# Low parts on another engine, and a shorter chain of sums and stores, in a one-core encoder layer

## The chip, the cores and the metric

The kernel runs on one core of a Trainium2 chip. A core has TensorE (matrix products, into the accumulator memory PSUM), VectorE, ScalarE and GpSimd (written POOL) for elementwise work, and SyncE (SP), which here only issues transfers. Each engine works through its own list of instructions in order, and semaphores tie the lists together. Transfers run on 16 DMA engines, which the lists of SP, ScalarE or POOL feed. The metric is the device time of one execution in microseconds (us).

## The reference: what is computed

One encoder layer for 512 positions of width 1024, all in float32 (shortened):

```python
x = x + 0.5 * swiglu(rms_norm(x, ffn1_norm), ffn1_w_gate, ffn1_w_up, ffn1_w_down)
h = rms_norm(x, mix_norm)
u = h @ w_in
f_out = fourier_mixer(u[..., :o0], fnet_w, fnet_b)
a_out = gqa_attention(u[..., o0:o1], u[..., o1:o2], u[..., o2:], q_norm, k_norm)
x = x + jnp.concatenate([f_out, a_out], axis=-1) @ w_out
x = x + 0.5 * swiglu(rms_norm(x, ffn2_norm), ffn2_w_gate, ffn2_w_up, ffn2_w_down)
return rms_norm(x, final_norm)
```

`swiglu(h, g, u, d)` is `(silu(h @ g) * (h @ u)) @ d`, with a hidden width of 2752. `rms_norm` divides each position by the root of the mean of its squares over the 1024 channels and multiplies by a gain per channel. The change touches the first FFN and the end of the second one with the final norm.

## The kernel before, in words

**Layout.** The activations lie with channels on the 128 partitions: `x[k]` is chunk k of the channels (8 chunks), 128 x 512. A norm's sum over the channels is therefore a product with a vector of ones.

**Exact products.** A float32 operand is split into a high part, rounded to the form that TensorE multiplies in one pass, and a low part, the rest. A product takes three passes (lines 108 to 110, or line 330): high by high, high by low, low by high. The high part is a cast, mostly on ScalarE. The low part is made in one of two ways. `lows` (line 71) is one VectorE subtraction. `rest_by_dma` (lines 89 to 92) has ScalarE write the negated high part into the low part's place, and then POOL issue a transfer that adds the source onto it:

```python
nc.scalar.activation(lo, asf(hi), AF.Copy, scale=-1.0)
nc.gpsimd.dma_start(out=lo, in_=src, accum_op=ALU.add)
```

**The first FFN's opening.** The hidden chunks come in groups (`GROUPS`). Most gate and up products go by a scheme with seven products of half size for eight (`seven`). It needs h in blocks and seven combinations of them, made by `operands` (lines 242 to 263) in four pairs i = 0 to 3: VectorE writes the scaled blocks of h into a tile b (line 248, two instructions a pair), and differences into a tile t (line 255); ScalarE casts b and t to high parts in `rt` (line 258); then come the low parts. For b in the first FFN that is `rest_by_dma`, for t and for the second FFN `lows`. The tile b has two buffers, so pair 2 takes the buffer of pair 0 when all that read it are done, a transfer included. Meanwhile TensorE runs the first gate and up blocks as plain products (`gate`), each weight block with a high and a low part in two slots of a ring; from the fourth block on these low parts come by `rest_by_dma` too (lines 100, 91, 92), straight from the weights in HBM. So POOL's queue holds transfers for weight blocks and for b in turn. `evacuate` (lines 489 to 510) takes the blocks' results out of PSUM. After the last plain block come the down products of the first group, then the seven products of the next.

**The end.** The last three output chunks of the second FFN (d = 5, 6, 7) are made in two halves of positions by `closing`: first positions 0 to 255 for all three, then positions 256 to 511. After each, `residual` (line 416, VectorE) adds the product to x and `square` (line 134, ScalarE) squares it. The sums of squares of the earlier chunks lie in `n3.acc`. For the first half, the tile acc and two tiles of squares are summed with `ones` (line 157): two columns of 128 positions, three tiles, two passes each. A float32 product without the split takes two passes. This and the mean (line 164, VectorE), the power -1/2 (line 171, POOL), and the copy to a wide tile (line 176) are `column`, which stands between the products of the second half, after their third step of 18. Each step has three passes. `finish` stands after the eighth step: transposes (line 184), a copy to `rb` (line 186, ScalarE), six multiplies by VectorE (line 965) and two by POOL for chunks 2 and 3 (line 963), and four stores of two chunks each in the order 0, 2, 4, 6, all issued by SP (line 968). For the second half, acc and the square of d = 6 are summed ahead of the last square, then the last square; each of the two columns has a PSUM bank and a mean of its own; then come the power, `rows` (products with the identity, lines 196 and 197), and again the multiplies and four stores.

**What sets the order.** Inside the two FFNs the orders of TensorE and SP are as written in the program (`in_order`). The orders of VectorE, ScalarE and POOL are set by a planner that fills each engine by a model of the times and the order of the program; it may place any instruction of these engines anew when any part of the program changes.

Of the kernel before, what the change touches and what calls it, by code (L numbers as in the profile page):

```python
# [8 lines left out]
BF16 = mybir.dt.bfloat16  # L9
# [4 lines left out]
P = 128  # L14
S = 512
D = 1024
KD = D // P
# [25 lines left out]
def encoder(ctx, tc, A, out):  # L43
    nc = tc.nc
# [7 lines left out]
    def bank(name):  # L52
        return pp.tile([P, S], F32, tag="bank", name=name)
# [3 lines left out]
    xt = cp.tile([P, KD, S], F32, name="xt")  # L57
# [12 lines left out]
    def lows(lo, src, hi):  # L70
        nc.vector.tensor_tensor(out=lo, in0=src, in1=asf(hi), op=ALU.subtract)  # L71
# [17 lines left out]
    def rest_by_dma(lo, hi, src):  # L89

        nc.scalar.activation(lo, asf(hi), AF.Copy, scale=-1.0)
        nc.gpsimd.dma_start(out=lo, in_=src, accum_op=ALU.add)
# [19 lines left out]
    class Norm:  # L112
# [39 lines left out]
            self.power(c0, c1)  # L152
            self.spread(c0, c1)

        def sum(self, ps, c, parts, first=True, last=True):
            for i, p in enumerate(parts):
                nc.tensor.matmul(
                    ps[:, 2 * c : 2 * c + 2], p[:, c * P : (c + 1) * P], ones,
                    start=first and i == 0, stop=last and i == len(parts) - 1,
                )  # L160

        def mean(self, ps, c0, c1):
# [17 lines left out]
        def row(self, c0=0, c1=4):  # L180

            ps = bank(f"rp{self.n}_{c0}")
            for c in range(c0, c1):
                nc.tensor.transpose(ps[:, c * P : (c + 1) * P], self.wide[:, c, :], ident)
            t = slice(c0 * P, c1 * P)
            nc.scalar.copy(self.rb[:, t], ps[:, t])
            return ps

        def rows(self, c0, c1):
# [8 lines left out]
            return pss[0]  # L198

    def ffn(norm, after, wgu, wd, wdt, opening, closing):  # L200

        n_ = norm.n
        n_plain = len(GROUPS[0])
        with tc.tile_pool(name=f"act{n_}", bufs=1) as ap, tc.tile_pool(name=f"sums{n_}", bufs=2) as sp:
# [36 lines left out]
            def operands(rp, i0, i1):  # L244
                for i in range(i0, i1):
                    b = sp.tile([P, 4, HALF], F32, tag="raw_g", name=f"b{n_}_{i}")
                    for o, k in ((0, i), (2, i + KH)):
                        nc.vector.scalar_tensor_tensor(
                            out=b[:, o : o + 2].rearrange("p a b -> p (a b)"), in0=x[k],
                            scalar=gains[:, norm.n, k : k + 1], in1=rp, op0=ALU.mult, op1=ALU.mult,  # L250
                        )
                    b12, b11, b22, b21 = (b[:, o] for o in range(4))
                    t = sp.tile([P, 4, HALF], F32, tag=("s12", "s34")[i % 2], bufs=1, name=f"t{n_}_{i}")
                    for o, (p, q) in enumerate(((b12, b11), (b22, t[:, 0]), (b22, b12), (b21, t[:, 1]))):
                        nc.vector.tensor_tensor(out=t[:, o], in0=p, in1=q, op=ALU.subtract)
                    for src, c in ((b[:, 1:], slice(0, 3)), (t, slice(3, 7))):
                        h, l = rt[:, c, 0, i], rt[:, c, 1, i]
                        nc.scalar.copy(h, src)
                        if src is t or n_:
                            lows(l, src, h)  # L260
                        else:
                            rest_by_dma(l, h, src)
# [158 lines left out]
            for gi, group in enumerate(GROUPS):  # L421
                last = gi == len(GROUPS) - 1
# [3 lines left out]
                else:  # L426
# [3 lines left out]
                    pss = dict(enumerate(opening(gate, lambda: norm.column([norm.acc]), lambda: row.append(norm.row()))))  # L430
                    back(lent[:2])
                    due, parts, left = [*pss, "t"], list(range(KH)), range(2 * len(pss), 2 * n_plain)
# [25 lines left out]
                for d in range(KD):  # L458
                    if last and closing and d == KD - 3:
                        closing([(e, down(e, group, gi)) for e in range(d, KD)], residual)  # L460
                        break
                    if last and d == KD - 2:
                        back(lent)
                    ps = bank(f"dn{n_}_{d}_{gi}")
                    steps = down(d, group, gi)(ps, every)
                    for _ in range(len(group) - (last and d < 2)):
                        next(steps)
                    waiting.append((d, ps, steps))
                    if d == 1 and not last:
                        ready = prepare(GROUPS[gi + 1][0] + 1)  # L470
                        ahead.extend(ready[1])
                    if d == 0:
                        rest()
                        if last:

                            lent = slots[KD - 2 : KD]
                            plain[2:2] = lent
                            continue
                    for d_, ps, steps in waiting:
                        for _ in steps:  # L480
                            pass
                        added(d_, ps)
                    waiting = []
# [49 lines left out]
    ident = cp.tile([P, P], F32, name="ident")  # L533
# [39 lines left out]
    with tc.tile_pool(name="mix", bufs=1) as mp, tc.tile_pool(name="mixt", bufs=1) as mt:  # L573

        more = mp.tile([P, 2, KD * P], F32R, name="more")
        more = [more[:, i, :] for i in range(2)]
# [26 lines left out]
        banks, rots, sqs = {}, {}, {}  # L603
# [191 lines left out]
        prob, parts, outs, pair, zs = {}, {}, {}, {}, {}  # L795
# [123 lines left out]
        def attend(n):  # L919
# [7 lines left out]
            if n >= 6:  # L927
                values(*at(n - 6))

        whole = sum(c for c, _, _ in fill)  # L930
        done = 0.0
        for n in range(38):
# [7 lines left out]
        for d in range(KD):  # L940
            whi, wlo = weights(A["wo"][d], f"o{d}")
            ps = bank(f"out{d}")
# [8 lines left out]
    n3 = Norm(3)  # L951

    ready = (2, 3)

    def finish(c0, c1, row=n3.row):

        t = slice(c0 * P, c1 * P)
        pr = row(c0, c1)
        for k0 in range(0, KD, 2):
            for k in (k0, k0 + 1):  # L960
                y = x[k][:, t]
                if k in ready:
                    nc.gpsimd.tensor_tensor(out=y, in0=y, in1=n3.rb[:, t], op=ALU.mult)
                else:
                    nc.vector.scalar_tensor_tensor(
                        out=y, in0=y, scalar=gains[:, 3, k : k + 1], in1=pr[:, t], op0=ALU.mult, op1=ALU.mult
                    )
            nc.sync.dma_start(out=out[:, k0 : k0 + 2, t], in_=xt[:, k0 : k0 + 2, t])

    def closing(downs, residual):  # L970

        for k in ready:
            nc.scalar.activation(x[k], x[k], AF.Copy, scale=gains[:, 3, k : k + 1])
        t0, t1 = slice(0, S // 2), slice(S // 2, S)
        sqs = []

        def more(sq, t):
            nc.vector.tensor_tensor(out=n3.acc[:, t], in0=n3.acc[:, t], in1=sq[:, t], op=ALU.add)

        for d, steps in downs:  # L980
            ps = bank(f"last{d}0")
            for _ in steps(ps, t0):
                pass
            residual(d, ps, t0)
            sq = n3.square(d, t0)
            if d == downs[0][0]:
                more(sq, t0)
            else:
                sqs.append(sq)
        i = 0  # L990
        for d, steps in downs:
            ps = bank(f"last{d}1")
            for _ in steps(ps, t1):
                i += 1
                if i == 3:
                    n3.column([n3.acc, *sqs], 0, 2)
                if i == 8:
                    finish(0, 2)
            if d < KD - 1:
                residual(d, ps, t1)  # L1000
                sq = n3.square(d, t1)
                if d == downs[0][0]:
                    more(sq, t1)
        pss = [bank(f"ss3_{c}") for c in (2, 3)]
        for c, pc in zip((2, 3), pss):
            n3.sum(pc, c, [n3.acc, sq], last=False)
        residual(KD - 1, ps, t1)
        sq = n3.square(KD - 1, t1)
        for c, pc in zip((2, 3), pss):
            n3.sum(pc, c, [sq], first=False)  # L1010
        for c, pc in zip((2, 3), pss):
            n3.mean(pc, c, c + 1)
        n3.power(2, 4)
        finish(2, 4, n3.rows)

    with in_order():
        ffn(n2, n3, A["wgu2"], A["wd2"], A["wdt2"], lambda gate, column, row: [[gate(0, {KD - 1: column}), gate(1, {3: row})]], closing)
# [104 lines left out]
```

## Time and profile before

| what | value |
|---|---|
| three runs | 880.9, 881.03, 880.14 us; median 880.9 us |
| the profiled execution | 880.02 us, of which the span from the first to the last instruction is 878.0 us |
| granted TensorE clock | 0.996 of full speed over the span |
| busy share | PE 98%, DVE 73%, ACT 52%, POOL 4% |
| transfers through POOL's queue | 2560 packets, 4.99 MB |
| bytes moved | 89.25 MB, 102 GB/s on average |

The profile is of one execution. PE is TensorE and PEld its weight loads, DVE is VectorE, ACT is ScalarE; SPq and POOLq are the parts of these engines that issue transfers and wait on semaphores. A line of the order of time has the start and the length in us, the engine, the line of the kernel, the operation, the tiles written and read, the shapes and the count; in brackets follows how long the engine stood idle just before, and what ended that. A line of the waits has who waited for whom, the total in us, the times and the longest. A line of the page's groups has the busy time in us and the mean of one in ns, and behind the second bar the idle time before them and what ended it. Ends of TensorE's passes are modelled.

### The profile page before, as it was taken

Reading aid. Unit: us, or ns where it says so; the run is one execution under the profiler, and the core shown is the slowest. Engines: PE = TensorE matmul, PEld = TensorE weight load, DVE = VectorE, ACT = ScalarE, POOL = GpSimd, SP = SyncE. Lnnn points to the kernel's source line nnn. Section 1 sums busy time; section 2 is a strip of 40 time slices with the busy share of each in tenths; the row PEclk is TensorE's granted clock in tenths of the full one; section 3 lists DMA queues with packets and bytes.
Section 4 is the critical chain, followed back from the end, with each engine's and each line's share of the span. In section 5 each row is a group of like instructions: output and inputs, shape, how many; then the busy total and the mean of one; then the engine's idle time right before and its main releaser. Section 6 shows DMA issues by size and latency. Waiting matters only on the chain.

```text
span 878.0 us, 13599 instructions
## 1 busy us (share of the span) xinstructions
PE 862.1 (98%) x5394; PEld 768.8 (88%) x5394; DVE 637.2 (73%) x1005; ACT 459.6 (52%) x761; POOL 31.7 (4%) x37
## 2 busy tenths in 40 slices
PE   8999999999999999999999999999999999999996
PEld 5878998899989998888888888889998999889986
DVE  7697985488746837699888558987974688459553
ACT  7773664256524644667775445535652366326441
POOL 0210000000000000211000000000000000000001
PEclk9999999999999999999999999999999999999998
DMA  7873322323243113521110213232323232332212
GB/s 245 199 163 135 142 85 67 120 97 119 75 143 110 46 51 108 204 84 37 49 49 25 90 63 136 84 132 97 109 78 126 95 118 78 102 115 84 73 37 96
DMA packets 31328, 89.25 MB, mean 102 GB/s; under 512 B 3616, under 2 KB 9248, under 8 KB 31136
## 3 DMA queue, kind: packets, MB, share of 16 engines
q1 hardware_dynamic: 28560, 83.37, 27.9%
q0 software_dynamic: 2560, 4.99, 3.0%
q8 instruction: 42, 0.69, 0.3%
q14 instruction: 22, 0.18, 0.1%
q10 hardware_dynamic: 144, 0.02, 0.0%
HBM read 83.91 MB, written 2.10 MB: 98 GB/s over the span
## 4 chain that ended last, share of the span: by engine, by line
PE 50%; issue 39%; DVE 5%; DMA 2%; ACT 2%; POOL 0%; SPq 0%; DVEq 0%; POOLq 0%; ACTq 0%
PE r L330 11%; PE q L330 6%; PE dn L108 4%; PE dn L110 4%; PE dn L109 4%; PE p L330 3%; PE out L108 2%; PE out L110 2%; PE out L109 2%; PE gu L110 1%; PE pt L816 1%; PE gu L108 1%; PE gu L109 1%; DMA rt<-b 1%; DMA ring<-in_wgu 1%
## 5 line engine op out<-in xcount | busy, mean ns | idle before, releaser
L330 PE MATMUL r<-rt,ring 128*128 128x256 f32 x1632 | 213.2, 283 | 0.1
L330 PEld LDWEIGHTS r<-rt,ring 128*128 128x128 f32 x1632 | 201.8, 188 | 2.6 <-ACT u L338 0.3
L108 PE MATMUL dn<-at,ring 128*128 128x512 f32 x303 | 119.7, 395 | 0.0
L109 PE MATMUL dn<-at,ring 128*128 128x512 f32 x303 | 119.6, 395 | 0.0
L110 PE MATMUL dn<-at,ring 128*128 128x512 f32 x303 | 119.6, 395 | 0.0
L330 PE MATMUL q<-rt,ring 128*128 128x256 f32 x816 | 107.9, 281 | 0.0
L330 PEld LDWEIGHTS q<-rt,ring 128*128 128x128 f32 x816 | 101.6, 188 | 0.0
L416 DVE SCALAR_TENSOR_TENSOR xt<-dn,xt 128x512 f32<-128x512 f32 x61 | 41.9, 688 | 80.1 <-PE dn L110 80.1
L71 DVE TENSOR_TENSOR ring<-s,ring 128x1024 fp32r<-128x1024 f32 x68 | 82.8, 1220 | 17.8 <-PE r L330 10.8
L100 ACT CAST ring<-raw_dn 128x768 fp32r<-128x768 f32 (+1 forms) x59 | 45.5, 775 | 95.2 <-PE dn L109 80.7
L291 ACT CAST ring<-s 128x1024 fp32r<-128x1024 f32 x68 | 71.4, 1050 | 40.3 <-PE r L330 18.3
L110 PEld LDWEIGHTS dn<-at,ring 128*128 128x128 f32 x303 | 57.0, 188 | 13.6
L109 PEld LDWEIGHTS dn<-at,ring 128*128 128x128 f32 x303 | 57.0, 188 | 13.0
L108 PEld LDWEIGHTS dn<-at,ring 128*128 128x128 f32 x303 | 57.0, 188 | 13.0
L71 DVE TENSOR_TENSOR ring<-raw_dn,ring 128x768 fp32r<-128x768 f32 (+1 forms) x59 | 51.7, 879 | 6.8 <-ACT ring L100 5.8
L71 DVE TENSOR_TENSOR ring<-raw_g,ring 128x1024 fp32r<-128x1024 f32 x34 | 41.6, 1222 | 17.0 <-PE p L330 11.0
L330 PE MATMUL p<-rt,ring 128*128 128x256 f32 x408 | 53.9, 281 | 0.0
L330 PEld LDWEIGHTS p<-rt,ring 128*128 128x128 f32 x408 | 50.8, 188 | 0.0
L291 ACT CAST ring<-raw_g 128x1024 fp32r<-128x1024 f32 x34 | 35.7, 1049 | 22.4 <-PE r L330 8.0
L300 ACT CAST ring<-raw_u 128x512 fp32r<-128x512 f32 x34 | 21.1, 621 | 37.1 <-PE dn L110 17.9
L110 PE MATMUL gu<-ring 128*128 128x512 f32 x96 | 37.9, 395 | 2.6 <-DMA ring<-in_wgu 1.8
L108 PE MATMUL gu<-ring 128*128 128x512 f32 x96 | 37.9, 395 | 0.8 <-ACT ring L553 0.7
(324 smaller groups left out, 1574.0 us busy)
## 6 DMA issues: line engine op xcount, KB each, us to landing
raw_dn<-in_wd SPq DMA_DIRECT2D x48, 384.0 KB, 3.0
raw_g<-in_wgu SPq DMA_DIRECT2D x34, 512.0 KB, 3.7
raw_u<-in_wgu SPq DMA_DIRECT2D x34, 512.0 KB, 4.4
raw_gu<-in_wgu SPq DMA_DIRECT2D x14, 512.0 KB, 3.5
raw_o<-in_wo SPq DMA_DIRECT2D x8, 512.0 KB, 3.5
raw_dn<-in_wd SPq DMA_DIRECT2D x16, 192.0 KB, 2.4
raw_in<-in_wins SPq DMA_DIRECT2D x6, 512.0 KB, 3.7
raw_f<-in_winf SPq DMA_DIRECT2D x4, 512.0 KB, 3.6
```

What stands on the lines that cost most here:

```text
L71: nc.vector.tensor_tensor(out=lo, in0=src, in1=asf(hi), op=ALU.subtract)
L100: nc.scalar.copy(hi[:, :n, :], raw[:, :n, :])
L108: nc.tensor.matmul(ps, whi, mhi, start=first, stop=False)
L109: nc.tensor.matmul(ps, whi, mlo, start=False, stop=False)
L110: nc.tensor.matmul(ps, wlo, mhi, start=False, stop=last)
L291: nc.scalar.copy(hi, src)
L300: nc.scalar.copy(hi, src)
L330: nc.tensor.matmul(ps, a[:, ks], b[:, i], start=first and i == 0 and o == 0, stop=i == KH - 1 and o == 2, skip_group_check=not first,)
L416: nc.vector.scalar_tensor_tensor(out=x[d][:, t], in0=ps[:, t], scalar=0.5, in1=x[d][:, t], op0=ALU.mult, op1=ALU.add)
L816: nc.tensor.transpose(pt[:, c * P : (c + 1) * P], prob[t, b, c][:, kc * P : (kc + 1) * P], ident)
```

## The change

1. In `operands` the low parts of b for pairs 0 and 1 of the first FFN are made by `lows` on VectorE; pairs 2 and 3 keep the transfer.
2. In `closing`, the squares of the first half of all three chunks are added to acc by VectorE, so that the column sums one tile: four passes in place of twelve. The column moves from behind the third step to behind the fifth, `finish` from behind the eighth to behind the ninth.
3. For the second half, both columns of sums go into one PSUM bank, and one mean takes both. Two idle products of 256 columns (`awake(1)`) stand ahead of the sums of d = 6, and four (`awake(2)`) behind the last sums.
4. In `finish` the order of the chunk pairs is 0, 4, 2, 6, and the store of pair 2 is issued by ScalarE, the others by SP.

```diff
-        def sum(self, ps, c, parts, first=True, last=True):
+        def sum(self, ps, c, parts, first=True, last=True, **how):
...
-                        if src is t or n_:
+                        if src is t or i < 2 or n_:
                             lows(l, src, h)
                         else:
                             rest_by_dma(l, h, src)
...
-        for k0 in range(0, KD, 2):
+        for k0 in (0, 4, 2, 6):
...
-            nc.sync.dma_start(out=out[:, k0 : k0 + 2, t], in_=xt[:, k0 : k0 + 2, t])
+            queue = nc.scalar if k0 in ready else nc.sync
+            queue.dma_start(out=out[:, k0 : k0 + 2, t], in_=xt[:, k0 : k0 + 2, t])
+
+    def awake(n):
+
+        unit = ident.bitcast(BF16)
+        ps = bank("awake")
+        for _ in range(2 * n):
+            nc.tensor.matmul(ps[:, : 2 * P], unit[:, :P], unit, start=True, stop=True)
...
-            sq = n3.square(d, t0)
-            if d == downs[0][0]:
-                more(sq, t0)
-            else:
-                sqs.append(sq)
+            more(n3.square(d, t0), t0)
...
-                if i == 3:
-                    n3.column([n3.acc, *sqs], 0, 2)
-                if i == 8:
+                if i == 5:
+                    n3.column([n3.acc], 0, 2)
+                if i == 9:
                     finish(0, 2)
...
-        pss = [bank(f"ss3_{c}") for c in (2, 3)]
-        for c, pc in zip((2, 3), pss):
-            n3.sum(pc, c, [n3.acc, sq], last=False)
+
+        pc = bank("ss3_2")
+        for c in (2, 3):
+            n3.sum(pc, c, [n3.acc], first=c == 2, last=False, skip_group_check=True)
+        awake(1)
+        for c in (2, 3):
+            n3.sum(pc, c, [sq], first=False, last=False, skip_group_check=True)
         residual(KD - 1, ps, t1)
         sq = n3.square(KD - 1, t1)
-        for c, pc in zip((2, 3), pss):
-            n3.sum(pc, c, [sq], first=False)
-        for c, pc in zip((2, 3), pss):
-            n3.mean(pc, c, c + 1)
+        for c in (2, 3):
+            n3.sum(pc, c, [sq], first=False, last=c == 3, skip_group_check=True)
+        awake(2)
+        n3.mean(pc, 2, 4)
         n3.power(2, 4)
         finish(2, 4, n3.rows)
```

More of the change, by code (lines that the diff above doesn't have):

```diff
@@ L158, in sum @@
                     ps[:, 2 * c : 2 * c + 2], p[:, c * P : (c + 1) * P], ones,
-                    start=first and i == 0, stop=last and i == len(parts) - 1,
+                    start=first and i == 0, stop=last and i == len(parts) - 1, **how,
                 )
@@ L974, in closing @@
         t0, t1 = slice(0, S // 2), slice(S // 2, S)
-        sqs = []
         def more(sq, t):
```

## The prediction

> **What bounds the kernel now.** I read the page's busy shares first, then the idle columns of its groups, then the waits and the order of time of the two places that the change touches: the first FFN's opening (28 to 60 us) and the last 20 us.
>
> ```profile
> PE 862.1 (98%) x5394; PEld 768.8 (88%) x5394; DVE 637.2 (73%) x1005; ACT 459.6 (52%) x761; POOL 31.7 (4%) x37
> ...
> L110 PE MATMUL gu<-ring 128*128 128x512 f32 x96 | 37.9, 395 | 2.6 <-DMA ring<-in_wgu 1.8
> ```
>
> TensorE is busy for 98% of the span, so nothing moves the time but its passes, its few waits, and what lies after its last pass. The second line shows the longest wait that a transfer causes: 1.8 us, for a gate block's low part. The waits of 28 to 60 us and the order of time show where it begins:
>
> ```profile
> DVE b L248 <- DMA rt<-b: 3.3, 1, 3.3
> ...
> ACT rt L258 <- DVE b L248: 2.1, 1, 2.1
> ...
> PE gu L110 <- DMA ring<-in_wgu: 1.8, 1, 1.8
> ```
>
> ```profile
> 42.27 1.41 DVE L248 SCALAR_TENSOR_TENSOR b<-xt,gains,rp 128x512 f32<-128x512 f32 x2 [3.29 <-DMA rt<-b]
> ```
>
> ```profile
> 43.71 0.84 ACT L258 CAST rt<-b 128x768 fp32r<-128x768 f32 x1 [2.08 <-DVE b L248]
> 44.57 0.63 ACT L505 ACTIVATE g0p<-u0p 64x512 f32<-64x512 f32 x1
> 45.23 1.05 ACT L100 CAST ring<-raw_gu 128x1024 fp32r<-128x1024 f32 x1
> 46.18 0.84 ACT L91 ACTIVATE rt<-rt 128x768 fp32r<-128x768 f32 x1
> 46.93 0.82 ACT L258 CAST rt<-b 128x768 fp32r<-128x768 f32 x1
> 47.65 0.51 ACT L100 CAST at<-raw_dn 128x384 fp32r<-128x384 f32 x1
> 48.06 1.06 ACT L91 ACTIVATE ring<-ring 128x1024 fp32r<-128x1024 f32 x1
> ```
>
> ```profile
> 49.41 0.91 POOL L92 DMA_DIRECT2D ring<-in_wgu  x1 [0.83 <-ACT ring L91]
> ```
>
> ```profile
> 55.59 0.50 PE L110 MATMUL gu<-ring 128*128 128x512 f32 x1 [1.77 <-DMA ring<-in_wgu]
> ```
>
> The tile b has two buffers. Pair 2 of h's blocks needs pair 0's, whose low part is made by an accumulating transfer that still reads it; VectorE stands 3.29 us for it, ScalarE 2.08 us behind VectorE. From 43.71 ScalarE runs without a gap to the negated copy (48.06) that the last gate block's transfer needs; that goes out at 49.41, lands at about 55.55, and TensorE has stood 1.77 us.
>
> At the end, one column of sums takes 12 passes between products, and after the last product a chain runs through every engine:
>
> ```profile
> 860.43 0.28 PE L157 MATMUL ss<-ones,acc 128*128 128x2 f32 x2
> 860.57 0.59 PE L157 MATMUL ss<-ones,sq 128*128 128x2 f32 x4
> 861.01 0.36 PE L157 MATMUL ss<-ones,acc 128*128 128x2 f32 x2
> 861.24 0.59 PE L157 MATMUL ss<-ones,sq 128*128 128x2 f32 x4
> 861.68 0.37 PE L108 MATMUL last<-at,ring 128*128 128x256 f32 x1
> ```
>
> ```profile
> 867.53 0.42 DVE L416 SCALAR_TENSOR_TENSOR xt<-last,xt 128x256 f32<-128x256 f32 x1 [0.38 <-PE last L110]
> 868.94 0.38 DVE L164 TENSOR_SCALAR ms<-ss 128x1 f32<-128x1 f32 x2 [0.98 <-PE ss L157]
> 870.90 2.44 DVE L965 SCALAR_TENSOR_TENSOR xt<-xt,gains,rp 128x256 f32<-128x256 f32 x6 [1.58 <-PE rp L196]
> ```
>
> ```profile
> 871.81 2.87 SPq L968 DMA_DIRECT2D out_y<-xt  x4
> ```
>
> The residual at 867.53 waits for TensorE, so whatever TensorE sheds before it shortens the end. The four stores leave one after another; the last is issued at 874.22.
>
> **The change, part by part.**
>
> *Low parts of pairs 0 and 1.* Removed: two negated copies on ScalarE (0.84 each), two transfers issued by POOL (1.30 and 1.34) with their data. Added: two VectorE subtractions of 128x768; rows of that shape (L71, ring<-raw_dn) take 0.96. What hides them is the 3.29 us that VectorE stands for the very transfer that goes: the work before it ends at 38.98, two subtractions bring it to 40.90, and pair 2 starts there instead of at 42.27, 1.37 us earlier (1.53 if one starts 0.08 before the other's record ends, as neighbouring rows do). Without that cover they would cost up to 1.92. ScalarE, relieved of 1.68, is free by then (its work ended at 41.62), so its seven gapless steps and POOL's issue move by as much. By the trace's semaphore events the copy at 45.23 needs a ring slot that TensorE leaves at 42.34, and the cast at 47.65 one that is free from 44.44, so neither holds the move back. The transfer lands at about 54.15; of the wait 0.4 is left. Gain 1.4. Bounds: 0, if the copy at 48.06 stays where it is for another reason, and 1.77, all there is. I take 1.4, since each link is a row. Late next is the down product at 60.7: its operands' last subtraction ends at 57.89, its third weight block's at 62.81 for a use at about 65.8; neither binds. After it VectorE is full from 60 to 70 us, but stands 0.74 and 3.02 us before the products at 80.9, and this work moves forward too.
>
> Here the trace and a rule part. POOL's issues of a gate block's transfer took 0.93 with VectorE mostly idle (26.57) and 0.87 with VectorE subtracting (34.26): no lock shows. The Trainium skill, "SBUF — State Buffer", section "SBUF: two separate sides", says that while VectorE runs an operation in a two-port mode GpSimd is locked out of the shared ports and cannot write its transfers' descriptors. By that rule each new subtraction could hold back an issue for about its length, and this part's sum would be about 0 instead of 1.4; whether a subtraction of this shape runs in such a mode, no row tells.
>
> *One accumulated tile, four passes.* 12 passes take 860.43 to 861.68, 0.104 each; eight fewer give 0.83. Two adds of 0.43 come onto VectorE where it stands 1.71 and 1.88 us; the second ends about 860.50 (the square's end) + 0.03 + 0.43 = 860.96. The column moves behind the fifth step, two steps of three passes of 0.119 later, to 861.14: it need not wait. Its mean comes at 861.7 instead of 861.86, the power (0.70) and the copy (0.29) end near 862.95, and the transposes, now behind the ninth step, come up at 863.0: a wait of up to 0.1. The residual that stood behind the copy (863.04) now goes ahead of it at 862.15, so the six multiplies start at about 863.55 instead of 864.38 and end near 866.0; the next residual follows at 866.0 and does not pass TensorE's last product at 866.7. The whole tail moves by 0.8. Bounds 0.4 (a wait on the copy or the add) and 0.9.
>
> *One mean.* The second of the two means starts as the last pass ends; that pass is still last. Gain 0 (between 0 and the 0.16 of one).
>
> *Idle products.* Two before the second sums, four behind the last. Products of the same 256 columns stand 0.119 apart here; the opening's idle products of 512 columns stand 0.42 apart, the slow end, so 0.21 for half. The two take 0.24 to 0.42, in a place where TensorE waits about 0.3 for the last square; the four 0.5 to 0.84, inside the 1.03 us that it waits for POOL. The granted clock is 1.00 up to 871 us, so there is no slow pass to mend. Cost 0, bounds -0.1 and 0.3.
>
> *Stores.* SP's issues took 0.37 to 0.46 and came at 871.81, 873.24 (behind POOL's pair, which ended at 873.21), 873.71, 874.22; each landed 2.06 to 2.46 us later. Now SP sends 0, 4, 6 as VectorE finishes them, the last at 873.37, and ScalarE, with nothing behind it in its queue, sends POOL's at 873.24. In the first half ScalarE has two squares behind that store, but POOL's pair ends about 865.5 there and the first square is ready at 866.4. Issue gains 0.85. But 256 KB at the 386 GB/s of 875 to 876 us take 0.68, and two stores now start together: the last lands about 873.24 + 2.14 + 0.68 = 876.06, against 876.68. Gain 0.6; bounds 0 and 0.85.
>
> Sum: 1.4 + 0.8 + 0.6 = 2.8 us. The profiled execution took 880.02 (878.0 span and 2.0 around it), so it would take 877.2; the median shown, 880.9, lies 0.9 above it, and 2.8 below that is 878.1.
>
> **Rivals.**
>
> The wait stays. ScalarE's and VectorE's orders are not written by hand; the copy at 48.06 stands three steps behind the cast that it reads, where the two blocks before had one step between; the trace gives no reason, so it may stay where it is when pair 2 comes earlier. For it: that unexplained place. Against: every row before it is gapless. Time 880.9 - 1.4 = 879.5.
>
> Transfers held back by the new work. If POOL cannot issue while VectorE subtracts, two rows of 0.96 hold the queue back by up to 1.92, more than the 1.4 won; the wait is then about what it was, and the time 879.5 again. For it: POOL's transfers run one behind another here. Against it: the two issue rows above. (It is what the skill's rule on the shared ports would make of this kernel.)
>
> The other side: an order made anew. New VectorE work shifts the order in which ScalarE and VectorE are filled, also where no line changed. The place is attention, 403 to 470 us, where TensorE already waits 3.5 us for ScalarE (1.4, 1.2, 0.5, 0.4). If these came to three times that, the time is 880.9 - 2.8 + 7.0 = 885.1; it decides for slower from 4.6 us of new waits, and hides the gain from 1.0. For it: those waits have hardly any slack. Against: if only the moment of that stage moves, its order stays.
>
> **How the numbers follow.** Runs spread from 880.14 to 881.03, so about 0.2%, 1.8 us, can be told from none. Forecast 0.60, all faster; the wait stays 0.18 and the transfers held back 0.05, both within 0.2%; a new order 0.17, of which 0.10 slower and 0.07 within. So faster 0.60, same 0.30, slower 0.10. The range: below, 1.77 + 0.9 + 0.85 off gives 877.4, and 0.9 more if the runs come at the profiled execution's level, 876.5; above, 881.2 takes in both cases of no change and the mild part of a new order; it leaves out about 0.15. The forecast's own range is 877.0 to 879.1.
>
> **What would show it.** Right: no wait of VectorE at L248 for a transfer of rt, pair 2 near 40.9, POOL's last gate issue near 48.0, TensorE's wait at the last gate block under 0.6; four L157 passes near 861.1; the last residual near 0.8 sooner from the tail's start; last store issued right behind the last multiply. Wrong: that gate issue still at 49.4, new waits of TensorE between 400 and 470 us, a wait ahead of L157 or L184, or squares behind ScalarE's store.

## The result, and the profile after

The changed kernel takes 876.8 us (median of six executions, 876.57 to 877.63), the kernel before in the same session 880.5 us (879.71 to 882.28). The ratio is 0.9957, with an interval of 0.9945 to 0.9970: 3.7 us faster, where 2.8 were forecast. The profiled execution took 877.63 us with a span of 875.5; it is the slowest of the six (the others have spans of 874.4 to 874.8), and the end of this section shows where it lost part of that.

The page's busy shares and its group of low-part products in the opening:

```profile
PE 862.5 (99%) x5392; PEld 768.5 (88%) x5392; DVE 640.0 (73%) x1008; ACT 458.8 (52%) x759; POOL 29.0 (3%) x35
...
L110 PE MATMUL gu<-ring 128*128 128x512 f32 x96 | 37.8, 394 | 0.7 <-DVE ring L71 0.7
```

The 1.8 us that these products stood for a transfer are gone; what is left is an old 0.7 for VectorE, early in the opening.

**The opening.** VectorE in order of time (start, length, line, tiles):

```profile
35.95 0.95 DVE L71 TENSOR_TENSOR rt<-b,rt 128x768 fp32r<-128x768 f32 x1
...
37.76 0.95 DVE L71 TENSOR_TENSOR rt<-b,rt 128x768 fp32r<-128x768 f32 x1
...
40.84 0.75 DVE L248 SCALAR_TENSOR_TENSOR b<-xt,gains,rp 128x512 f32<-128x512 f32 x1
```

The two new low parts take 0.95 each, and pair 2's b follows at 40.84 without any wait; 40.90 was predicted. ScalarE behind it:

```profile
42.44 1.05 ACT L100 CAST ring<-raw_gu 128x1024 fp32r<-128x1024 f32 x1 [0.36 <-PE gu L109]
43.40 0.83 ACT L258 CAST rt<-b 128x768 fp32r<-128x768 f32 x1
44.13 1.05 ACT L91 ACTIVATE ring<-ring 128x1024 fp32r<-128x1024 f32 x1
```

This is not the old order moved forward. The last gate block's cast now stands ahead of pair 2's, and its negated copy follows one step later instead of three. So POOL's issue comes much sooner than a shift of 1.4 us would bring it:

```profile
45.48 0.86 POOL L92 DMA_DIRECT2D ring<-in_wgu  x1 [5.17 <-ACT ring L91]
47.43 1.30 POOL L92 DMA_DIRECT2D rt<-b  x1 [1.09 <-ACT rt L91]
```

It was 49.41 before and 48.0 in the prediction. The transfer lands at 50.86 by its semaphore events, about 3 us ahead of TensorE, which takes the low part without standing:

```profile
53.97 0.39 PE L110 MATMUL gu<-ring 128*128 128x512 f32 x1
```

How much that is worth is read by setting the same TensorE pass of both traces side by side. Up to the last gate block the changed kernel lies 0.31 later. (That is not the change: in six other kernels with the same opening this is between -0.08 and 0.22.) From the second pass behind the old wait on it lies 1.73 earlier. The step is 2.04 us, more than the 1.77 that the bracket showed: passes follow each other every 0.23 there although a record lasts 0.39, so the 2.16 between the starts at 53.43 and 55.59 held 1.93 of loss, and the pass behind the wait took 0.11 longer. At the start of the last half 1.47 of the 1.73 is left, lost in small steps and at no new wait; attention's waits, where a rival had put its price, are as they were:

```profile
PE o L835 <- ACT ph L819: 1.4, 2, 0.9
PE f L726 <- ACT e L810: 1.2, 1, 1.2
...
PE s L803 <- ACT e L810: 0.5, 1, 0.5
PE pt L816 <- ACT e L810: 0.4, 1, 0.4
```

**The end.** TensorE at the column of the first half:

```profile
859.67 0.50 PE L157 MATMUL ss<-ones,acc 128*128 128x2 f32 x4
860.03 0.37 PE L108 MATMUL last<-at,ring 128*128 128x256 f32 x1
```

Four passes, no wait ahead of them, and none ahead of the transposes at 861.54. From the first product of the last half to its last took 7.00 us (857.89 to 864.89), before 7.85 (859.36 to 867.21): 0.85 saved, 0.83 predicted. From the last product to the identity products it is 2.94 in both (864.89 to 867.83, 867.21 to 870.15), so the single mean brought nothing, as predicted. TensorE from the last product on:

```profile
865.00 0.51 PE L157 MATMUL ss<-ones,acc 128*128 128x2 f32 x4
865.37 0.38 PE L976 MATMUL awake<-ident 128*128 128x256 bf16 x2
865.74 1.06 PE L157 MATMUL ss<-ones,sq 128*128 128x2 f32 x8
866.66 0.60 PE L976 MATMUL awake<-ident 128*128 128x256 bf16 x4
867.83 1.82 PE L196 MATMUL rp<-ident,r 128*128 128x128 f32 x8 [0.57 <-POOL r L171]
```

The idle products fit into TensorE's waits, but here they did not do what they could: the granted clock fell to half at 868.14, and the eight identity products took 1.82 us instead of the 1.16 of before, where the clock fell only at 871.65. The products took 0.66 longer in this one execution. VectorE could start its multiplies only 1.00 us after the first of them instead of 0.75, and from the first of them to the end of the span it is 7.63 us, where an execution of `awake_more` (below), with the same stores and the clock held, took 7.22: about 0.4 lost. The last stores are issued by SP until 871.67 and by ScalarE at 871.57.

Between the two profiled executions alone the difference is 2.5 us (878.0 and 875.5 of span), less than the 3.7 of the medians, because the late opening, the small steps and the slow end (together about 1 us) fell into this execution.

### The profile page after: what moved, and what is told of

The parts are those of the page before. It is cut to its first block, busy times and chain, and to the rows that moved or that the text cites. A ratio compares the mean times of both kernels' runs of the same rounds, so it can differ in the third digit from the quotient of the medians.

```text
span 875.5 us, 13587 instructions
## 1 busy us (share of the span) xinstructions
PE 862.5 (99%) x5392; PEld 768.5 (88%) x5392; DVE 640.0 (73%) x1008; ACT 458.8 (52%) x759; POOL 29.0 (3%) x35
## 4 chain that ended last, share of the span: by engine, by line
PE 94%; DVE 1%; ACT 1%; DMA 1%; issue 1%; SPq 0%; POOL 0%; POOLq 0%; DVEq 0%; ACTq 0%
PE r L330 22%; PE q L330 11%; PE dn L110 8%; PE dn L108 8%; PE dn L109 8%; PE p L330 6%; PE gu L110 4%; PE gu L108 4%; PE gu L109 4%; PE out L108 2%; PE out L110 2%; PE out L109 2%; PE pt L816 1%; PE q L108 1%; PE q L109 1%; PE q L110 1%
```

## Experiments

Each experiment's kernel was timed beside the kernel before, in three sets, each on a chip of its own. The kernel before had a median of 882.34 us in the first set (29 executions), 882.77 in the second (9) and 881.82 in the third (21), against 880.52 in the comparison above. So a ratio is to be set against others of its set only. No set timed the changed kernel itself again; where an expectation speaks of it, the nearest kernel of the set, or the comparison above, stands in for it. "Pass by pass" below is the comparison of the same TensorE pass in two traces, as above; the trace of before is one of a fast execution (880.02 us).

### First set: which part, and what the wait hangs on

**Part 1 alone** (`low_only`, made from the kernel before) and **everything but part 1** (`end_only`, made from the changed kernel; it takes this edit back):

```diff
-                        if src is t or n_:
+                        if src is t or i < 2 or n_:
```

> Part 1 alone: the low parts of pairs 0 and 1 by VectorE, the end as before. The theory (the two parts add up): TensorE's 1.77 us wait for the last gate block's transfer is gone, the last 20 us are as before, and the time is 1.8 to 2.0 us below before (878.6). Rival, an order made anew elsewhere: the difference is found in attention (403 to 470 us), where TensorE's waits of 3.5 us change, and the time differs from that by more than 0.7 us.

> Parts 2, 3 and 4 alone: pairs 0 and 1 keep their transfers. The theory: the wait of 1.77 us stays, the span from the last half's first product to the last product shortens by 0.86 us as in the changed kernel, the stores give 0.6 more, and the time is 1.4 to 1.7 us below before (879.0). Rival: the two parts don't add up, and what this one and part 1 alone give sums to over 0.8 us more or less than 3.7 us.

Part 1 alone: 878.37 us, ratio 0.9959 (0.9946 to 0.9972), 4.0 us less, where 1.8 to 2.0 were expected; its time is near the 878.6 expected, it is the kernel before that is slower in this set. Pass by pass against the profile of before it gains 2.1 at the last gate block and holds it to the end. The rest: 880.79 us, ratio 0.9983 (0.9975 to 0.9992), 1.55 less, against 0.85 for the column and 0.6 for the stores. The wait is still there:

```profile
55.73 0.50 PE L110 MATMUL gu<-ring 128*128 128x512 f32 x1 [2.00 <-DMA ring<-in_wgu]
```

So the end is as large as worked out. The two parts sum to 5.5 us, 1.8 more than the 3.7 of the comparison above, which the expectation had named as the sign that they don't add up. But 1.8 is also what the kernel before is slower by in this set, and the second set's kernels near the changed one are 5.4 to 6.0 below theirs: within a set the parts add up as far as can be told. Part 1 is worth 2.1 by the records, but 4.0 by these medians; that gap is taken up in the third set. One piece of it may be seen here. The opening of `end_only` is that of the kernel before, but in its trace a load of weights (raw_g) lets ScalarE go on only at 60.23, before at 58.83. VectorE, in the same order, runs its next subtractions 1.4 later, and TensorE loses 0.9 more at the down products from 65 to 82 us. The profile of before has no such loss; how often its other executions have it is not known.

**A buffer of its own for pair 2's b** (`b_own`, from the kernel before; two kept tiles go down to one buffer each to make room):

```diff
-                    b = sp.tile([P, 4, HALF], F32, tag="raw_g", name=f"b{n_}_{i}")
+                    own = {"tag": "b2", "bufs": 1} if i == 2 and not n_ else {"tag": "raw_g"}
+                    b = sp.tile([P, 4, HALF], F32, name=f"b{n_}_{i}", **own)
```

> Before, with pair 2's tile b in a buffer of its own (two of the seven-product scheme's temporary tiles of the first FFN get one buffer less to make room); all four low parts stay transfers. Theory of the buffer: VectorE no longer stands 3.3 us before pair 2, the last gate block's copy and transfer go out 1 to 4 us sooner, the wait of 1.77 us falls under 0.6, and the time is 1.2 to 1.9 us below before. Rival theory, of the queue (what helped is that 5.2 us of transfers left POOL's queue): the queue is as full as before, the last gate block's transfer still lands about 55.5 us, and the time is within 0.5 us of before.

It took 884.88 us, ratio 1.0025 (1.0013 to 1.0037): 2.5 slower, which no theory had. Pair 2's b indeed waits no longer, but the planner now sends the b transfers ahead of the gate blocks' in POOL's queue:

```profile
40.60 1.25 POOL L92 DMA_DIRECT2D rt<-b  x1 [0.94 <-ACT rt L91]
42.07 0.91 POOL L92 DMA_DIRECT2D ring<-in_wgu  x1 [0.22 <-issue]
48.55 1.27 POOL L92 DMA_DIRECT2D rt<-b  x1 [5.58 <-ACT rt L91]
50.02 0.92 POOL L92 DMA_DIRECT2D ring<-in_wgu  x1 [0.20 <-issue]
```

and TensorE waits at the last two gate blocks, which costs 1.4 us more than before at each:

```profile
50.72 0.50 PE L110 MATMUL gu<-ring 128*128 128x512 f32 x1 [1.13 <-DMA ring<-in_wgu]
...
59.60 0.50 PE L110 MATMUL gu<-ring 128*128 128x512 f32 x1 [3.14 <-DMA ring<-in_wgu]
```

Then something new comes. Windows of 2 us (TensorE's busy time and count, weight loads, VectorE, ScalarE, POOL, the granted clock, the DMA engines' share, GB/s):

```profile
60.00:62.00 2.00, 2.00 (x8) 1.57 (x7) 0.79 (x1) 1.80 (x3) 0.00 (x0) 0.66 0.00 0
62.00:64.00 2.00, 2.00 (x6) 1.57 (x5) 2.00 (x4) 0.29 (x1) 0.00 (x0) 0.50 0.00 0
```

Right behind the wait of 3.14 the granted clock is half, from 60.62 to 64.03 us, though TensorE is busy all the time: six passes in 2 us where there were ten. Pass by pass this alone loses about 1.6 us. So a wait can be paid twice. This is the second slowest of the twelve executions, and its opening came 1.2 us late as well; the 2.5 of the medians is about what the two waits cost. (The run does not tell the theories of the first wait apart, since the edit moved the whole queue.)

**The last gate block's low part by VectorE** instead of by transfer (`last_gate`, from the kernel before):

```diff
-                        pss.setdefault(c // 2, []).append(gate(c, by_dma=not n_))
+                        pss.setdefault(c // 2, []).append(gate(c, by_dma=not n_ and c != left[-1]))
```

> Before, with the last gate block's low part by a VectorE subtraction (1.22 us) in place of the transfer; the pairs keep theirs. It prices the disputed wait by itself. If that wait is all that part 1 is worth: TensorE stands under 0.3 us there, and the time is 1.6 to 2.0 us below before, as part 1 alone. If part 1 gives more than the wait (a shorter queue, an earlier start of the seven products), this one gives at least 0.5 us less than part 1 alone.

880.83 us, ratio 0.9986 (0.9977 to 0.9995), 1.5 less. The wait is gone there too (2.0 gained pass by pass), but VectorE is then late with the down product's weights:

```profile
65.43 0.50 PE L110 MATMUL dn<-at,ring 128*128 128x512 f32 x1 [1.14 <-DVE ring L71]
```

1.3 us are lost there and 0.5 at the next such pass. Relieving POOL's last transfer at VectorE's cost where VectorE is full is worth less than doing it where VectorE stands waiting.

### Second set: the end

All four are made from the changed kernel. **No idle products** (`no_awake`, both lines left out) and **twice as many** (`awake_more`):

```diff
-        awake(1)
+        awake(2)
...
-        awake(2)
+        awake(4)
```

> The changed kernel without its idle products. Theory (they are worth nothing): the median is within 0.2 us of the changed kernel's; where the granted clock falls before the last products with the identity, it depends on the phase of a window of 3.41 us in either kernel. Rival (they hold the clock): more executions run those products at half clock, eight passes taking 1.8 us in place of 1.1, and the median is 0.4 to 0.9 us above the changed kernel's.

> The changed kernel with four idle products in place of two, and eight in place of four. Theory: median within 0.2 us of the changed kernel's, since eight of 0.11 us end before the power is there (0.9 us of 1.17). Rival (they hold the clock): no execution drops before the last products, all spans lie within 0.3 us of each other, and the median is up to 0.3 us lower.

Without them 877.19 us, ratio 0.9939 (0.9926 to 0.9951); with twice as many 876.97 us, ratio 0.9937 (0.9925 to 0.9949). The identity products of each:

```profile
867.24 2.08 PE L196 MATMUL rp<-ident,r 128*128 128x128 f32 x8 [1.03 <-POOL r L171]
```

```profile
867.42 1.16 PE L196 MATMUL rp<-ident,r 128*128 128x128 f32 x8
```

Without them the clock fell at 866.88 and the products ran at half speed throughout; with twelve it fell at 870.51, behind them, and every execution's mean clock was 0.998 or 0.999 (0.995 to 0.997 without). With six it fell at 868.14 in the profiled execution of the changed kernel, behind the first two of them, but behind all of them in the profiles of `stores_old`, `order_only` and `column_3`. The mean clocks of all executions say it more surely. Of the 28 of kernels with neither idle products nor the wait in the opening (`low_only`, `last_gate`, `pair_0`, `no_awake`) none is above 0.997; of the 20 with six products (the changed kernel and the three just named) 12 are; of the five with twelve all are. So idle products do hold the clock, and doubled they hold it better. In the median `no_awake` is 0.2 us above `awake_more` and 0.4 above `order_only` (below), which has six; the ranges of five executions overlap, so a worth of up to about 0.4 is not clear of the scatter. The medians settle neither the theory's 0.2 nor the rival's 0.4.

**Stores as before** (`stores_old`: order 0, 2, 4, 6, all by SP) and **the new order, all by SP** (`order_only`, which has the second of these edits alone):

```diff
-        for k0 in (0, 4, 2, 6):
+        for k0 in range(0, KD, 2):
...
-            queue = nc.scalar if k0 in ready else nc.sync
+            queue = nc.sync
```

> The changed kernel with part 4 undone: pairs in the order 0, 2, 4, 6, all stores from SP. As predicted: the last store is issued 0.85 us later after the last multiply begins, and the time is 0.6 us (0.3 to 0.85) above the changed kernel's. Rival (the data's time sets the end): the last store lands within 0.2 us of the changed kernel's, and so does the time.

> The changed kernel with the new order 0, 4, 2, 6 but all stores from SP. If the order is what counts: the store of POOL's pair goes third and the last right after it, the last issue is 0.4 to 0.5 us later than in the changed kernel, but the data of 256 KB takes 0.66 us a store, so the time is 0 to 0.3 us above. If the second queue is what counts: 0.4 us or more above.

877.38 us, ratio 0.9943 (0.9930 to 0.9955), and 876.77 us, ratio 0.9936 (0.9922 to 0.9949). SP's four issues in the old order, and then in the new one:

```profile
869.75 2.87 SPq L969 DMA_DIRECT2D out_y<-xt  x4
```

```profile
869.48 2.35 SPq L969 DMA_DIRECT2D out_y<-xt  x4
```

From the first identity product to the end of the span it is 7.80 us in the old order and 7.19 in the new one: 0.6, all from the order, as between the medians. With the second queue (seen in `awake_more`, whose identity products also ran at full speed) it is 7.22. There the last issue comes 3.22 us after the first identity product, with one queue 3.54 after it; but the last store lands 5.94 after it with two queues and 5.90 with one. The Trainium skill, "DMA: Bandwidth & Descriptors", section "Issuing engines are not separate DMA queues", says that issuing from several engines saves only the time of the issue itself. The trace agrees: 0.3 saved at the issue, nothing at the landing.

### Third set: buffer or queue, the wait's second price, the column's place

**Only pair 0 by VectorE** (`pair_0`) and **pairs 2 and 3 in place of 0 and 1** (`pairs_23`), both from the kernel before, with `i == 0` and `i > 1` for `i < 2` in the line of part 1. They part the two readings of part 1: pair 2's b gets its buffer sooner, or POOL's queue has fewer transfers ahead of the gate block's.

> Before, with the low part of pair 0 alone by VectorE: pair 2 has its buffer without a transfer, and POOL's queue keeps its order (the last gate block behind pair 2). Theory of the buffer, as predicted: pair 2 starts 1.4 to 2.5 us sooner, the last gate block's issue moves as much, the wait falls to 0.6 us or less, and the time is 2.5 to 4 us below before. Theory of the queue: with pair 2's transfer still ahead, the wait stays at 1 us or more, and the time is at most 2 us below.

> Before, with the low parts of pairs 2 and 3 (not 0 and 1) by VectorE. Pair 2 must still wait for pair 0's transfer, so the buffer is held as before, while in POOL's queue no pair stands between the last two gate blocks. Theory of the queue: VectorE still stands about 3.3 us before pair 2, yet the last gate block's transfer, alone in the queue, lands 2 us and more sooner; TensorE's wait there is under 0.3 us, and the time is 3 to 4 us below before, as with part 1 alone. Theory of the buffer: with the 3.3 us the copy and the issue stay near 48 to 49.4 us, a wait of 1 us or more stays, and the time is at most 1 us below before.

Pair 0 alone: 879.01 us, ratio 0.9960 (0.9946 to 0.9973), 2.8 less. VectorE:

```profile
40.01 1.40 DVE L248 SCALAR_TENSOR_TENSOR b<-xt,gains,rp 128x512 f32<-128x512 f32 x2
42.62 1.41 DVE L248 SCALAR_TENSOR_TENSOR b<-xt,gains,rp 128x512 f32<-128x512 f32 x2 [1.20 <-DMA rt<-b]
```

and POOL:

```profile
44.52 1.27 POOL L92 DMA_DIRECT2D rt<-b  x1 [4.46 <-ACT rt L91]
46.19 0.91 POOL L92 DMA_DIRECT2D ring<-in_wgu  x1 [0.41 <-ACT ring L91]
```

Pair 2 is free at 40.01, the gate block's transfer is issued at 46.19 still behind pair 2's, lands at 52.46, and TensorE does not wait (2.0 gained pass by pass). Pairs 2 and 3: 882.02 us, ratio 0.9999 (0.9991 to 1.0008). There VectorE waits as before, the issue stays where it was, and so does the wait:

```profile
42.80 1.41 DVE L248 SCALAR_TENSOR_TENSOR b<-xt,gains,rp 128x512 f32<-128x512 f32 x2 [3.68 <-DMA rt<-b]
```

```profile
39.66 0.88 POOL L92 DMA_DIRECT2D ring<-in_wgu  x1 [1.21 <-ACT ring L91]
49.27 0.86 POOL L92 DMA_DIRECT2D ring<-in_wgu  x1 [8.73 <-ACT ring L91]
```

```profile
55.22 0.50 PE L110 MATMUL gu<-ring 128*128 128x512 f32 x1 [1.27 <-DMA ring<-in_wgu]
```

The transfer issued at 39.66 had landed by 46.98, so POOL's queue was empty when the gate block's transfer was issued at 49.27, and it still took 5.9 us to land. The queue theory falls; the time of the issue counts, and that hangs on pair 0's buffer.

**The wait filled with idle products** (`filled_wait`, from the kernel before). This asks for the second price of the wait that `b_own` showed: 16 idle products on the last gate block's own bank, ahead of its first product, keep TensorE busy while the wait lasts.

```diff
+                if c == 7 and not n_:
+                    unit = ident.bitcast(BF16)
+                    for _ in range(16):
+                        nc.tensor.matmul(ps[:, : 2 * P], unit[:, :P], unit, start=True, stop=True)
```

> Before, with 16 idle products of 256 columns (1.7 us) ahead of the last gate block's first product. Nothing lands sooner, TensorE only works through most of the time in which it would stand. If the wait has a second price, a fall of the granted clock behind it in some of the executions: none has a mean clock under 0.995, and the median is 0.8 to 1.8 us below before. If the scatter of before comes from elsewhere (the transfers' own times): the clocks and times scatter as before, the median within 0.4 us.

882.7 us, ratio 1.0011 (1.0002 to 1.0020): 0.9 slower, where a gain was expected. TensorE shows why this figure can't be read alone:

```profile
53.26 1.92 PE L225 MATMUL gu<-ident 128*128 128x256 bf16 x16
54.94 0.48 PE L108 MATMUL gu<-ring 128*128 128x512 f32 x1
55.25 0.40 PE L109 MATMUL gu<-ring 128*128 128x512 f32 x1
55.77 0.50 PE L110 MATMUL gu<-ring 128*128 128x512 f32 x1
...
69.92 0.50 PE L110 MATMUL dn<-at 128*128 128x512 f32 x1 [0.74 <-DVE at L71]
...
81.27 0.50 PE L110 MATMUL dn<-at,ring 128*128 128x512 f32 x1 [0.86 <-DVE ring L71]
```

The idle products fill the wait at a cost of 0.18 (55.77 against 55.59). But the planner set VectorE's work anew, and pass by pass 0.9 is lost at 69.92 and 1.0 at 81.27, waits that the profile of before does not have. Taken off, the median is some 1.1 below the kernel before: the size expected, but with a correction as large as the effect, so by its time this run settles nothing.

The mean granted clocks of all executions of the three sets say more. 27 of the 59 executions of the kernel before have a mean clock of 0.994 or less, and their median is 883.04 us; the 18 with 0.996 or more have 881.29. The difference of 1.75 is about one stretch of 3.41 us at half clock (1.71 us, and 0.002 of the mean). Over all kernels with the wait at the last gate block (the kernel before, `end_only`, `b_own`, `pairs_23`) 42 of 94 executions are so low. With the wait filled it is 1 of 11. Over the kernels without it, the changed one among them, it is none of 53. (The idle products at the end raise the mean clock of some of these kernels; but among the kernels with the end of before it is 39 of 82 with the wait and none of 23 without.) `last_gate` fits: by its last such wait it is only 0.3 ahead pass by pass, but its median is 1.5 lower, and none of its 12 executions is so low in clock. So the wait has a second price, paid in part of the executions: a fall of the clock. The link of wait and mean clock is measured; that the fall lies right behind this wait is seen in one profile only, of `b_own`, where the wait was longer. The profiles of before, `end_only` and `pairs_23` have a wait of 1.27 to 2.00 us and no fall behind it, so which executions pay, and whether their wait was longer, stays open.

**The column at its old place** (`column_3`, from the changed kernel):

```diff
-                if i == 5:
+                if i == 3:
...
-                if i == 9:
+                if i == 8:
```

> The changed kernel with the column behind the third step and the transposes behind the eighth, as before, but one tile to sum. As predicted, the last add ends about 0.55 us after the column comes up there, so TensorE stands 0.4 to 0.6 us before the first pass of the column, and the products of the last half take that much longer than in the changed kernel: 0.3 to 0.6 us above it. If the add is earlier than worked out: no wait and the same time as the changed kernel.

877.92 us, ratio 0.9953 (0.9939 to 0.9966). TensorE and then VectorE:

```profile
859.91 0.61 PE L157 MATMUL ss<-ones,acc 128*128 128x2 f32 x4 [0.42 <-DVE acc L985]
```

```profile
859.43 0.42 DVE L985 TENSOR_TENSOR acc<-acc,sq 128x256 f32<-128x256 f32 x1 [0.55 <-ACT sq L134]
```

The pass ahead starts at 859.21 and its successor would start 0.12 later; the column starts at 859.91, so 0.58 is lost, and the last half takes 7.64 us instead of 7.00. The add ends at 859.85 and TensorE stands for it. The median is 1.1 above that of the comparison, more than the 0.3 to 0.6 expected, but it is of four executions in another set; the trace shows the 0.6. With the column left where it was, two thirds of what the eight passes save would have gone into that wait.

## Why the prediction was right, and where its terms were off

The likeliest case came: 878.1 forecast, 876.8 measured, inside the range and 0.2 below the forecast's own range. That the range held it is in part luck: the gain of 3.7 us is above the 3.5 that the upper bounds of its three terms add up to, and the time is inside because the lower end had 0.9 more for the level of the runs. Term by term:

- **Low parts of pairs 0 and 1.** The mechanism held: pair 2 at 40.84 (40.90 predicted), the two subtractions hidden under VectorE's wait, the whole driven by pair 0's buffer (`pair_0` against `pairs_23`). The size was off: 1.4 against 2.04 pass by pass. Two steps failed. "Its seven gapless steps and POOL's issue move by as much" replayed the old order; the planner made a new one and the issue came 3.9 us sooner instead of 1.4. And the upper bound of "1.77, all there is" was too low, since the bracket counts from the modelled end of the pass ahead.
- **One tile, four passes.** 0.85 against 0.8. The adds and the move behind the fifth step were read rightly: `column_3` shows the wait of 0.58 that the move avoids.
- **One mean.** 0 predicted, 0 found (2.94 us in both traces).
- **Idle products.** Cost 0, as predicted. But the reason "there is no slow pass to mend" was wrong: it took the one profile, in which the clock fell at 871.65, for the rule. In `no_awake` it fell at 866.88, ahead of the identity products, in the changed kernel at 868.14, among them.
- **Stores.** 0.6 in size, but the cause was only half right: the order gives all of it. The last issue came 0.84 sooner (0.85 predicted), 0.32 of that by sending pair 2 from ScalarE, but that part moved no landing.

By the records the sum is 2.04 + 0.85 + 0.6 = 3.5, against 3.7 between the medians of that comparison. In the second set kernels that differ little from the changed one are up to 6.0 below the kernel before (`order_only`), because the kernel before was slower there. The chip as a whole was not: `order_only` and `awake_more` took 876.8 and 877.0 there, the changed kernel 876.8 in the comparison. So what was slower belongs to the kernel before. The second price of the wait explains up to 1.7 of that difference for an execution, and the late load seen in `end_only` might add 0.9. How the rest comes about stays open.

**The rivals.** The wait did not stay. New orders came, in the opening rather than in attention, and for the better; `filled_wait`, `b_own` and `last_gate` show the same planner turning small edits into new or longer waits of 0.3 to 3.1 us, so the doubt was sound and only its sign was open. Transfers held back by VectorE did not show, but the new subtractions (35.95 to 36.90, 37.76 to 38.71) met no issue of POOL (34.57, 39.44), so they put the rule on the shared ports (the Trainium skill, "SBUF — State Buffer", section "SBUF: two separate sides") to no test; the one subtraction that did overlap an issue, at 39.90, left that at 0.86.

No kernel of the experiments clearly beats the changed one: the medians of `order_only` and `awake_more`, in another set, lie within 0.2 us of it.

## What to carry to other kernels

Follow a wait of the bounding engine back through every queue to the buffer that starts it, and put the replacing work on the engine that stands waiting there; a like subtraction put where that engine is full (`last_gate`) came back as another wait. Where a planner orders the engines, the old order replayed gives the mechanism but not the size. And a single profile shows one phase of the clock: compare the mean clocks of many executions before calling a wait's idle time its whole price.

## What the runs showed of the hardware

- **The clock falls on a grid.** Across these kernels' profiles, the stretch of full clock up to its fall at the end was 856.75, 860.16, 863.57, 866.99 or 870.40 us long: steps of 3.41. The Trainium skill, "TensorE: Matmul & The Clock Gate", section "What's actually happening", describes a free-running window of about 3.4 us, and half clock after an idle one; the trace agrees in the length. In `b_own` one step at half clock breaks it, behind 51.20 us of full clock, fifteen steps. Which share of a window makes it idle no run settles. The step before 868.14 of the changed kernel counted as idle though TensorE's records fill 2.84 of its 3.41 us, with passes of two columns and six idle products. In `b_own` TensorE's records fill 1.02 of the step before 60.62. But the wait of 1.77 in the profile of before lay whole within one step (52.45 to 55.87, counted back from 871.65), the rest of it filled with products of 512 columns, and no fall followed.
- **The mean clock leaves out the opening.** In five of the fourteen profiles (`low_only`, `no_awake`, `awake_more`, `b_own`, `pairs_23`) TensorE's passes of 512 columns stand 0.43 us apart until 9 to 10 us, as they did in `b_own` at half clock from 60.62 on; in the others they reach 0.23 before 7 us. At 12 us these five lie 1.0 to 1.2 us behind the kernel before; two us later all but `b_own` have come within 0.15. The mean clock of 0.993 of `b_own` is accounted for by the two later stretches at half clock alone (3.41 us, and the 8.2 from 876.41 to the end).
- **An accumulating transfer takes about as long from an empty queue.** 512 KB of a gate block took 5.4 us from issue to landing in the changed kernel and 5.9 in `pairs_23`, both with nothing under way ahead of it; 6.1 before and 6.3 in `pair_0`, both right behind another transfer; and 9.5 in `b_own`. The DMA engines were full there for most of that time (0.92 to 1.26 in windows of 2 us), but no less so before (1.06 to 1.18), so what made it 9.5 stays open.
